# Two modulation groups of a diffusion backbone moved from between two groups of the input projection into the second of them

## The chip, the cores and the metric

The kernel runs on one core of one Trainium2 chip. The metric is the device time of one execution in microseconds (us), the median of three runs. Within a core, TensorE (PE in the profile) multiplies matrices, VectorE (DVE), ScalarE (ACT) and GpSimd (POOL) work on elements, and queues move data by DMA. SyncE (SP) only issues DMAs here. Each engine takes its instructions in the order of its own program and waits for the others by semaphores.

## The reference

Two layers work on 512 latent tokens and 256 context tokens of width 1024. Each layer begins with a modulation: the conditioning vectors `c` and `c_ctx` go through SiLU and a matrix `w_mod` of 1024 x 6144, which gives shift, scale and gate for the mixer and again for the experts. The normalised and modulated tokens `h` are then multiplied by `w_in` (1024 x 1536), and the columns of the product feed pooling, a spatial gating unit and attention:

```python
sh1, sc1, g1, sh2, sc2, g2 = modulation(c, w_mod[l], b_mod[l])
hl = modulate(x, sh1, sc1)
zl = hl @ w_in[l]
ql = apply_rope(rms_norm(heads(zl, OFF_Q, N_HEADS), q_g[l]), cos, sin)
kl = apply_rope(rms_norm(heads(zl, OFF_K, N_KV_HEADS), k_g[l]), cos, sin)
attn_l = block_attention(ql, jnp.concatenate([kl, kc], axis=1), jnp.concatenate([vl, vc], axis=1))
yl = mixer_output(zl, attn_l, pool_w[l], pool_scale[l], sgu_g[l], sgu_w[l], sgu_b[l], w_out[l])
```

After the mixer come a residual, a layer norm and a mixture of 16 experts. In the last layer the context tokens are only needed as keys and values.

## The kernel before

The input projection is done in three groups of 512 columns: first keys, values and the pooling columns, then the queries, then the two halves of the gating unit. `project(g, ...)` does the second and the third. It walks over eight slices k of the 1024 inputs. In each step ACT rounds the weight slice to the short format (`whi`, L223), DVE subtracts that from the weight (`wlo`, L224), and PE multiplies every tile of 128 tokens three times (L228 to L230): high by high, low by high, high by low. Layer 0 has six token tiles, so 18 products of 512 columns for each k; layer 1 has four tiles and 12 products. `whi` and `wlo` have two buffers each. The sums stay in PSUM (tiles `s`, two tiles of tokens each, `po` and `bk`) until all eight steps are done; then `evacuate` copies them, for the second group to `zq`.

While one group is multiplied, `prepare(k)` lets waiting generators take a step. During the second group these are the keys (L549 turns them into `kT`); during the third, the queries and the pooling. A query of one token tile is a chain: square (ACT L648), reduce (DVE L650), scale (DVE L191), power -0.5 (POOL L193, `qr`), multiply (DVE L653), multiply by the two rotary tables (POOL L657 and DVE L658), add (DVE L663), round (ACT L668), subtract the rounded part (DVE L669), eight transposes on PE (L675), and two copies to `qT`. After them the pooling multiplies a band matrix (L577). Attention begins with the scores (L750).

`mod_group` computes 512 columns of the modulation for both conditioning vectors. It loads two halves of `w_mod`, multiplies them in 16 matmuls (printed as two rows of four for each half's share, L153), and copies the result by ACT. A gate goes to `gpart` (L164) and its bias arrives by DMA. A shift or scale goes to `mpart` (L168), is transposed by PE in four pieces (L174) and summed by DVE (L175, L177). Two such groups stand in `mixer` between the second and the third group of the projection: in layer 0 one gate and one shift, in layer 1 two shifts.

Weights come in halves of 1 MB into a pool of four buffers (`ring`); in layer 1 a second pool of three (`ring1`) is added. SP issues the loads in the order of the program text; a load waits until its buffer has been read for the last time. The other engines' orders are made by a list scheduler, which moves instructions of one engine past each other where their data allow it.

Of the kernel before, what the change touches and what calls it, by code (L numbers as in the profile page):

```python
# [44 lines left out]
def step(gens, n=1):  # L45

    while n and gens:
        if next(gens[0], None):
            n -= 1
        else:  # L50
            gens.pop(0)


class Net:
# [185 lines left out]
    def mixer(self, l, left, prev):  # L240

        nc, a = self.nc, self.a
        last = l == DEPTH - 1
# [70 lines left out]
        def bank(t, pss):  # L314
            if t < LT and t % 2 == 0:
                s2 = self.P("s2")
                pss[t], pss[t + 1] = s2[:, :512], s2[:, 512:]
            elif t >= LT:
                pss[t] = self.P("po" if t == LT else "bk")

        def multiply(k, t, pss, whi, wlo):
            if k == 0:
                bank(t, pss)
            n = 256 if (last and t >= LT) else 512
            tk = slice(128 * t, 128 * t + 128)
            if last and t >= LT:
                tk = slice(128 * (t - LT), 128 * (t - LT) + 128)
                hi, lo = ctx["hi"][:, k, tk], ctx["lo"][:, k, tk]
            else:
                hi, lo = self.cat(0, k, tk), self.cat(1, k, tk)  # L330
            self.mm3(pss[t][:, :n], hi, lo, whi[:, :n], wlo[:, :n], k == 0, k == KC - 1)

        raw1 = []
# [131 lines left out]
            for t in range(NT):  # L465
                evacuate(t, pss[t], 512 if t < LT else 256)

        def project(g, raw, prepare, evacuate):

            toks = list(range(LT if last else NT))  # L470
            pss = {}
            for k in range(KC):
                prepare(k)
                whi = self.T(wl, [128, 512], "whi", F32R, bufs=2)
                wlo = self.T(wl, [128, 512], "wlo", F32R, bufs=2)
                self.split(raw[k], whi, wlo)
                for t in toks:
                    multiply(k, t, pss, whi, wlo)
            for t in toks:
                evacuate(t, pss[t], 256 if (last and t >= LT) else 512)  # L480

# [20 lines left out]
        others = []  # L502
        if l == 0:
            others = [(l, g) for g in (4, 5, 6, 7, 8, 9)]
        else:
            others = self.spare
# [174 lines left out]
        early = [keys()]  # L681
# [5 lines left out]
        def evac1(t, ps, n):  # L687
# [2 lines left out]
                at["zq"] = self.T(pool, [128, NT, 512], "zq", bufs=1)  # L690
            plain(at["zq"])(t, ps, n)

        project(1, raw1, lambda k: step(early, 1), evac1)
        zq = at["zq"]
        ge = at["ge"] = self.T(pool, [128, NT, 512], "x12")
        band = at["band"] = self.T(pool, [128, 4, 5, 128], "y12")
        nc.gpsimd.dma_start(band, a["band"])
        for m in others[2:4] if last else others[1:3]:
            self.mod_group(*m)
        qT = {}  # L700
        early += [queries(t, qT, zq) for t in range(LT if last else NT)] + [pooling(*st) for st in streams]

        def evac2(t, ps, n):
            nc.scalar.activation(ge[:, t, :], ps, AF.Gelu_apprx_tanh)

        project(2, self.load_cols("w_in", l, 2, 0), ahead, evac2)
        step(early, 1000)
        wl_stack.close()
# [1116 lines left out]
```

## Time and profile before

| | us |
|---|---|
| median of three runs | 1758.88 (1757.2 to 1763.34) |
| the profiled execution | 1761.27 |
| its span in the profile | 1759.4 |
| PE busy | 1597.1 (91%) |
| DVE busy | 620.7 (35%) |
| ACT busy | 399.8 (23%) |
| POOL busy | 334.8 (19%) |

The span is the time from the first to the last instruction that the profiler saw. The change touches about 60 us of each layer: in layer 0 from about 93 us (the second group's fourth step) to 156 us, in layer 1 from about 1034 to 1093 us. The sums over the whole span say little on these; the rows further down are taken from them.

### The profile page before, as it was taken

Reading aid. Unit: us, or ns where it says so; the run is one execution under the profiler, and the core shown is the slowest. Engines: PE = TensorE matmul, PEld = TensorE weight load, DVE = VectorE, ACT = ScalarE, POOL = GpSimd, SP = SyncE. Lnnn points to the kernel's source line nnn. Section 1 sums busy time; section 2 is a strip of 40 time slices with the busy share of each in tenths; the row PEclk is TensorE's granted clock in tenths of the full one; section 3 lists DMA queues with packets and bytes.
Section 4 is the critical chain, followed back from the end, with each engine's and each line's share of the span. In section 5 each row is a group of like instructions: output and inputs, shape, how many; then the busy total and the mean of one; then the engine's idle time right before and its main releaser. Section 6 shows DMA issues by size and latency. Waiting matters only on the chain. (4 is left out here: it accounts for less than half of the span.)

```text
span 1759.4 us, 26138 instructions
## 1 busy us (share of the span) xinstructions
PE 1597.1 (91%) x10855; PEld 835.3 (47%) x10855; DVE 620.7 (35%) x1323; ACT 399.8 (23%) x766; POOL 334.8 (19%) x354
## 2 busy tenths in 40 slices
PE   6989999987899999999998788999599988988896
PEld 3767775763444444444443566877333322222222
DVE  4543663583111111111112945657522222122214
ACT  3333664143000000000001644653400001000001
POOL 2423210022211211211211432201101100101002
PEclk9999999997999999999999798999799999999998
DMA  9441008558999999999998554054899999999994
GB/s 332 152 173 49 1 25 317 188 227 312 368 400 400 392 400 399 391 401 400 391 400 292 196 205 146 1 198 180 321 407 408 408 409 409 408 409 409 408 409 193
DMA packets 159550, 525.09 MB, mean 298 GB/s; under 512 B 10517, under 2 KB 13589, under 8 KB 159177
## 3 DMA queue, kind: packets, MB, share of 16 engines
q1 hardware_dynamic: 146116, 487.37, 71.2%
q0 software_dynamic: 10720, 27.46, 5.3%
q10 hardware_dynamic: 2596, 8.59, 1.2%
q8 instruction: 86, 1.41, 0.3%
q14 instruction: 32, 0.25, 0.0%
HBM read 504.52 MB, written 18.87 MB: 297 GB/s over the span
## 5 line engine op out<-in xcount | busy, mean ns | idle before, releaser
L1330 PE MATMUL h<-ring,xT 128*64 128x512 f32 x1448 | 331.7, 602 | 22.6 <-DMA ring<-in_w 19.7
L1330 PEld LDWEIGHTS h<-ring,xT 128*64 128x64 f32 x1448 | 98.9, 137 | 228.0 <-issue 182.1
L1330 PE MATMUL y<-ring,gpart 128*64 128x512 f32 x792 | 182.1, 603 | 9.8 <-DMA ring<-in_w 8.2
L229 PE MATMUL s<-wlo,cat 128*128 128x512 f32 x352 | 143.1, 407 | 7.8 <-DVE wlo L224 7.5
L228 PE MATMUL s<-whi,cat 128*128 128x512 f32 x352 | 144.3, 412 | 5.2 <-ACT whi L885 2.5
L1330 PE MATMUL h<-cat,xT 128*64 128x512 f32 x600 | 138.5, 603 | 5.8 <-DMA cat<-in_w 5.4
L230 PE MATMUL s<-whi,cat 128*128 128x512 f32 x352 | 141.7, 403 | 0.5 <-POOL cat L433 0.5
L1640 POOL DMA_INDIRECT acc<-y,rows x32 | 51.2, 1601 | 393.3 <-DVE y L1639 393.0
L1330 PEld LDWEIGHTS y<-ring,gpart 128*64 128x64 f32 x792 | 54.7, 138 | 126.7 <-issue 110.2
L1349 ACT ACTIVATE hT<-tr 128x64 f32<-128x64 f32 x34 | 7.3, 225 | 415.6 <-DVE hT L1351 414.3
L1349 ACT ACTIVATE gpart<-tr 128x256 f32<-128x256 f32 x32 | 12.3, 384 | 310.2 <-DVE gpart L1351 310.1
L1330 PEld LDWEIGHTS h<-cat,xT 128*64 128x64 f32 x600 | 40.8, 138 | 88.3 <-issue 71.7
L229 PEld LDWEIGHTS s<-wlo,cat 128*128 128x128 f32 x352 | 68.0, 193 | 26.6 <-DVE wlo L224 10.8
L228 PEld LDWEIGHTS s<-whi,cat 128*128 128x128 f32 x352 | 67.8, 194 | 25.9 <-issue 3.9
L753 DVE TENSOR_REDUCE am<-s 128x1 f32<-128x768 f32 (+1 forms) x68 | 65.9, 969 | 34.7 <-PE s L750 34.4
L1435 DVE SCALAR_TENSOR_TENSOR half<-y,gates,g 64x512 f32<-64x512 f32 x28 | 21.0, 750 | 161.2 <-PE y L1330 160.9
L1330 PE MATMUL c<-ring,xT 128*32 128x256 f32 x1344 | 77.6, 380 | 0.0
L750 PE MATMUL s<-kT,qT 128*128 128x256 f32 (+1 forms) x288 | 70.8, 367 | 5.9 <-ACT zq L765 5.5
L230 PEld LDWEIGHTS s<-whi,cat 128*128 128x128 f32 x352 | 68.1, 194 | 15.7 <-POOL cat L433 0.9
L765 ACT ACTIVATE zq<-s,anm 128x768 f32<-128x768 f32 (+1 forms) x80 | 65.0, 816 | 28.0 <-DVE anm L755 27.5
L153 PE MATMUL bk<-ring,cc 128*32 128x512 f32 x384 | 50.7, 645 | 20.4 <-DMA ring<-in_w_mod 19.8
L799 PE MATMUL po<-y,Z 128*64 128x128 f32 x832 | 66.9, 285 | 2.1 <-DVE zt L816 2.1
(346 smaller groups left out, 2189.9 us busy)
## 6 DMA issues: line engine op xcount, KB each, us to landing
ring<-in_w SPq DMA_DIRECT2D x280, 1024.0 KB, 19.0
cat<-in_w SPq DMA_DIRECT2D x104, 1024.0 KB, 19.2
ring<-in_w_mod SPq DMA_DIRECT2D x48, 1024.0 KB, 8.1
ring<-in_w_in SPq DMA_DIRECT2D x12, 1024.0 KB, 8.1
ring<-in_w_out SPq DMA_DIRECT2D x8, 1024.0 KB, 10.6
tab<-nn ACTq DMA_DIRECT2D x10, 512.0 KB, 7.2
acc<-res ACTq DMA_DIRECT2D x6, 512.0 KB, 4.2
fin<-acc SPq DMA_DIRECT2D x6, 512.0 KB, 4.8
```

The source lines that it names most:

```text
L153: nc.tensor.matmul(ps[32 * t:32 * t + 32, :], self.sil[:, o:o + 32], wm[k], start=k < 4, stop=k >= 4)
L228: nc.tensor.matmul(ps, ahi, bhi, start=start, stop=False)
L229: nc.tensor.matmul(ps, ahi, blo, start=False, stop=False)
L230: nc.tensor.matmul(ps, alo, bhi, start=False, stop=stop)
L750: nc.tensor.matmul(sp[:, nk * m + b0:nk * m + b1], qT[t][:, 2 * j + h, :], kT[:, 2 * h + x, k0 + b0:k0 + b1], start=x == 0, stop=x == 1)
L753: nc.vector.tensor_reduce(mx, sp[:, :nk * n].rearrange("p (m k) -> p m k", k=nk), axis=AX.X, op=OP.max)
L765: nc.scalar.activation(pbuf[:, i % 3, nk * m:nk * m + nk], sp[:, nk * m:nk * m + nk], AF.Exp, bias=nm[:, m:m + 1], scale=QK_SCALE, accum_o ...
L799: nc.tensor.matmul(po[t][64 * h:64 * h + 64, 128 * j:128 * j + 128], Z0[:, c0 + c, 128 + 64 * h:192 + 64 * h], pT[:, 128 * c:128 * c + 128 ...
L1330: self.nc.tensor.matmul(outs[s][o:o + cap, :], stat[s][:, k, :], w[k][:, n * t:n * t + n], start=k == 0, stop=k == KC - 1)
L1349: nc.scalar.activation(o[:, r], pv[:, r], AF.Copy)
L1435: nc.vector.scalar_tensor_tensor(ys[j][(r + odd) % 2][p], y[p], gates[p, e:e + 1], g2[odd][p], op0=OP.mult, op1=OP.mult)
L1640: nc.gpsimd.indirect_dma_start(out=self.acc[l, s], out_offset=bass.IndirectOffsetOnAxis(ap=rows[:, e:e + 1], axis=0), in_=y, in_offset=Non ...
```

## The change

`project` takes a list of modulation groups and works one off after step k = 3 and one after step k = 5. The second group of the projection gets the two that stood behind it.

```diff
--- before.py
+++ after.py
@@ -465,8 +465,10 @@
             for t in range(NT):
                 evacuate(t, pss[t], 512 if t < LT else 256)
 
-        def project(g, raw, prepare, evacuate):
-
+        def project(g, raw, prepare, evacuate, mods=()):
+
+
+            mods = list(mods)
             toks = list(range(LT if last else NT))
             pss = {}
             for k in range(KC):
@@ -476,6 +478,8 @@
                 self.split(raw[k], whi, wlo)
                 for t in toks:
                     multiply(k, t, pss, whi, wlo)
+                if k in (3, 5) and mods:
+                    self.mod_group(*mods.pop(0))
             for t in toks:
                 evacuate(t, pss[t], 256 if (last and t >= LT) else 512)
 
@@ -690,13 +694,11 @@
                 at["zq"] = self.T(pool, [128, NT, 512], "zq", bufs=1)
             plain(at["zq"])(t, ps, n)
 
-        project(1, raw1, lambda k: step(early, 1), evac1)
+        project(1, raw1, lambda k: step(early, 1), evac1, others[2:4] if last else others[1:3])
         zq = at["zq"]
         ge = at["ge"] = self.T(pool, [128, NT, 512], "x12")
         band = at["band"] = self.T(pool, [128, 4, 5, 128], "y12")
         nc.gpsimd.dma_start(band, a["band"])
-        for m in others[2:4] if last else others[1:3]:
-            self.mod_group(*m)
         qT = {}
         early += [queries(t, qT, zq) for t in range(LT if last else NT)] + [pooling(*st) for st in streams]
```

The scheduler orders the engines anew. At the three places below the names end in running numbers, which differ between the two files; line numbers above 468 are four higher in the changed file within `mixer`.

PE in layer 0, after the products of the second group's fourth step (`bk_681` is the PSUM tile of the sixth token tile, `s_157` that of the first two). Before:

```order
L228 MATMUL bk_681<-whi_740,cat_208 128x512
L229 MATMUL bk_681<-wlo_741,cat_208 128x512
L230 MATMUL bk_681<-whi_740,cat_209 128x512
L549 MATMUL bk_762<-ident_70,zq_735 128x128 x4
L549 MATMUL bk_768<-ident_70,zq_735 128x128 x2
L228 MATMUL s_157_663<-whi_772,cat_205 128x512
L229 MATMUL s_157_663<-wlo_773,cat_205 128x512
```

And now:

```order
L228 MATMUL bk_681<-whi_740,cat_208 128x512
L229 MATMUL bk_681<-wlo_741,cat_208 128x512
L230 MATMUL bk_681<-whi_740,cat_209 128x512
L153 MATMUL bk_766<-ring_762,cc_66 32x512 x4
L153 MATMUL bk_766<-ring_764,cc_66 32x512 x4
L553 MATMUL bk_778<-ident_70,zq_735 128x128 x4
L228 MATMUL s_157_663<-whi_788,cat_205 128x512
L229 MATMUL s_157_663<-wlo_789,cat_205 128x512
L553 MATMUL bk_784<-ident_70,zq_735 128x128 x2
```

The first modulation group (L153) stands between two steps of the group, and the transposes of the keys move a little into the next step.

DVE in layer 0 at the first two queries of the third group (`qv_947` and `qr_949` belong to the first query, `qs_1000` and `qv_1002` to the second; `wlo_1028` is the weight part of the third group's second step). Before:

```order
L650 TENSOR_REDUCE qs_945<-zt_943 128x8
L561 COPY zq_890<-po_677 128x512
L191 TENSOR_SCALAR qv_947<-qs_945 128x8
L653 TENSOR_TENSOR zq_890<-zq_890,qr_949 128x512
L658 TENSOR_TENSOR zt_943<-zq_890,rt_639 128x512
L650 TENSOR_REDUCE qs_1000<-zt_998 128x8
L663 TENSOR_TENSOR zt_952<-zt_952,zt_943 128x512
L191 TENSOR_SCALAR qv_1002<-qs_1000 128x8
```

And now:

```order
L654 TENSOR_REDUCE qs_945<-zt_943 128x8
L565 COPY zq_929<-po_677 128x512
L191 TENSOR_SCALAR qv_947<-qs_945 128x8
L657 TENSOR_TENSOR zq_929<-zq_929,qr_949 128x512
L224 TENSOR_TENSOR wlo_1028<-ring_939,whi_1027 128x512
L662 TENSOR_TENSOR zt_943<-zq_929,rt_639 128x512
L654 TENSOR_REDUCE qs_1000<-zt_998 128x8
L667 TENSOR_TENSOR zt_952<-zt_952,zt_943 128x512
L191 TENSOR_SCALAR qv_1002<-qs_1000 128x8
```

The subtraction for `wlo_1028`, which stood behind the second query's operations, has moved between the first query's two multiplications.

DVE in layer 1, from the second query's multiplication (by `qr_8175`) to the third's (by `qr_8220`); `qq_8135` is the first query's rounded part, `qq_8182` the second's. Before:

```order
L653 TENSOR_TENSOR zq_8065<-zq_8065,qr_8175 128x512
L175 TENSOR_REDUCE cols_1450_8088<-bk_8111 128x8
L561 CAST qT_8138<-bk_8139 128x512
L177 TENSOR_TENSOR cols_1450_8088<-cols_1450_8088,bcol_75 128x8
L658 TENSOR_TENSOR zt_8169<-zq_8065,rt_7864 128x512
L650 TENSOR_REDUCE qs_8216<-zt_8214 128x8
L663 TENSOR_TENSOR zt_8178<-zt_8178,zt_8169 128x512
L191 TENSOR_SCALAR qv_8218<-qs_8216 128x8
L224 TENSOR_TENSOR wlo_8244<-ring_1457_8118,whi_8243 128x512
L653 TENSOR_TENSOR zq_8065<-zq_8065,qr_8220 128x512
```

And now:

```order
L657 TENSOR_TENSOR zq_8110<-zq_8110,qr_8175 128x512
L673 TENSOR_TENSOR qq_8135<-zt_8131,qq_8135 128x8x64
L662 TENSOR_TENSOR zt_8169<-zq_8110,rt_7864 128x512
L224 TENSOR_TENSOR wlo_8289<-ring_1457_8118,whi_8288 128x512
L565 CAST qT_8138<-bk_8139 128x512
L667 TENSOR_TENSOR zt_8178<-zt_8178,zt_8169 128x512
L654 TENSOR_REDUCE qs_8216<-zt_8214 128x8
L224 TENSOR_TENSOR wlo_8357<-ring_1458_8120,whi_8356 128x512
L673 TENSOR_TENSOR qq_8182<-zt_8178,qq_8182 128x8x64
L191 TENSOR_SCALAR qv_8218<-qs_8216 128x8
L657 TENSOR_TENSOR zq_8110<-zq_8110,qr_8220 128x512
```

The sums of the modulation (L175, L177) are gone from here, and two weight subtractions and two query subtractions have come in between the same two multiplications.

## Rows read from the trace of the kernel before

**Rows 1.** Busy us (count) of PE, PEld, DVE, ACT, POOL; granted clock; DMA; GB/s
```profile
112.00:125.00 13.00, 7.77 (x50) 3.85 (x45) 8.81 (x16) 5.69 (x10) 7.27 (x5) 0.87 0.83 301
125.00:156.00 31.00, 27.97 (x148) 22.39 (x148) 18.64 (x32) 10.13 (x18) 14.01 (x8) 1.00 0.14 44
```
**Rows 2.** Timeline of PE, layer 0: start, us, instruction [idle before it <-releaser]
```profile
56.37 1.92 PE L153 MATMUL bk<-ring,cc 128*32 128x512 f32 x16
58.22 1.22 PE L305 MATMUL bk<-ident,xh 128*128 128x128 f32 x6
...
111.85 3.64 PE L153 MATMUL bk<-ring,cc 128*32 128x512 f32 x32
118.84 0.66 PE L174 MATMUL bk<-ident,mpart 128*128 128x128 f32 x4 [3.35 <-ACT mpart L168]
120.95 1.23 PE L675 MATMUL bk<-ident,qq 128*128 128x128 f32 x8 [1.45 <-DVE qq L669]
...
124.54 0.50 PE L229 MATMUL s<-wlo,cat 128*128 128x512 f32 x1 [0.43 <-DVE wlo L224]
...
150.91 0.80 PE L675 MATMUL bk<-ident,qq 128*128 128x128 f32 x8
151.54 0.46 PE L228 MATMUL s<-whi,cat 128*128 128x512 f32 x1
...
155.79 2.41 PE L577 MATMUL bk<-y,Z 128*64 128x128 f32 x40
```
**Rows 3.** Timeline of PE, layer 1
```profile
1034.55 0.63 PE L549 MATMUL bk<-ident,zq 128*128 128x128 f32 x6
...
1047.81 1.93 PE L153 MATMUL bk<-ring,cc 128*32 128x512 f32 x16
1050.45 0.66 PE L174 MATMUL bk<-ident,mpart 128*128 128x128 f32 x4 [0.72 <-ACT mpart L168]
...
1055.22 0.50 PE L229 MATMUL s<-wlo,cat 128*128 128x512 f32 x1 [1.59 <-DVE wlo L224]
...
1076.58 0.87 PE L675 MATMUL bk<-ident,qq 128*128 128x128 f32 x8
...
1092.74 0.39 PE L230 MATMUL s<-whi,cat 128*128 128x512 f32 x1
1092.97 0.94 PE L750 MATMUL s<-kT,qT 128*128 128x512 f32 x4
```
**Rows 4.** Timeline of DVE, layer 0
```profile
114.35 0.69 DVE L653 TENSOR_TENSOR zq<-zq,qr 128x512 f32<-128x512 f32 x1 [1.79 <-POOL qr L193]
115.08 0.69 DVE L658 TENSOR_TENSOR zt<-zq,rt 128x512 f32<-128x512 f32 x1
...
119.51 0.69 DVE L653 TENSOR_TENSOR zq<-zq,qr 128x512 f32<-128x512 f32 x1 [1.78 <-POOL qr L193]
...
120.72 1.79 DVE L658 TENSOR_TENSOR zt<-zq,rt 128x512 f32<-128x512 f32 x1
...
144.63 0.69 DVE L653 TENSOR_TENSOR zq<-zq,qr 128x512 f32<-128x512 f32 x1 [0.56 <-POOL qr L193]
```
**Rows 5.** Timeline of POOL, both layers
```profile
112.66 1.66 POOL L193 TENSOR_TENSOR qr<-qv,mh 128x8 f32<-128x8 f32 x1 [24.54 <-DVE qv L191]
...
120.28 1.68 POOL L657 TENSOR_TENSOR zt<-zq,rt 128x512 f32<-128x512 f32 x1 [0.81 <-DVE zq L653]
...
132.32 2.12 POOL L193 TENSOR_TENSOR qr<-qv,mh 128x8 f32<-128x8 f32 x1 [1.49 <-DVE qv L191]
...
1058.20 1.30 POOL L657 TENSOR_TENSOR zt<-zq,rt 128x512 f32<-128x512 f32 x1 [0.87 <-DVE cols L175]
```
**Rows 6.** Timeline of DVE, layer 1
```profile
1051.18 0.69 DVE L653 TENSOR_TENSOR zq<-zq,qr 128x512 f32<-128x512 f32 x1 [1.78 <-POOL qr L193]
...
1071.34 0.69 DVE L653 TENSOR_TENSOR zq<-zq,qr 128x512 f32<-128x512 f32 x1 [0.57 <-POOL qr L193]
...
1075.83 0.69 DVE L669 TENSOR_TENSOR qq<-zt,qq 128x512 fp32r<-128x512 f32 x1 [0.15 <-ACT qq L668]
```
**Rows 7.** Tile ring, 1030 to 1060 us: from issue to landing of its loads
```profile
DMA to landing us min/median/max: 5.1/9.7/14.4
```

## The prediction

> **What bounds the kernel now.** I read the granted clocks first, then the busy time by stretch, then the timelines of TensorE (PE), VectorE (DVE) and GpSimd (POOL) around the two places where the second group of the input projection meets the third. [rows 1]: in layer 0 PE is busy 7.77 of the 13 us at the boundary, and 27.97 of the 31 us after it. So there is idle time for the change to win, and it is small: PE rows of layer 0 show waits of 3.35, 1.45 and 0.43 us [rows 2], of layer 1 0.72 and 1.59 us [rows 3]. That is 7.5 us of 1759.
>
> What ends those waits matters more than their size. After the boundary six queries (four in layer 1) go through a chain that alternates between engines: DVE makes the mean square, POOL raises it to the power -0.5 (L193, "qr"), DVE multiplies (L653), POOL and DVE each multiply by a table (L657, L658), DVE adds (L663), ACT rounds (L668), DVE subtracts (L669), and PE turns the result (L675). PE holds the turns in its fixed order among the products of the third group, so it can't run ahead of this chain. The L653 of the first and the last query of layer 0 start at 114.35 and 144.63 [rows 4]: five turns of the chain in 30.3 us, 6.1 each. The 18 products between the last turn and the pooling take 155.79 - 151.54 = 4.25 us, 0.236 each [rows 2]; a step of the loop with one turn (0.63) is thus 4.9 us. The chain is slower than the products. It bounds this stretch, and it can only start when the second group has ended.
>
> **The change part by part.** E is the start of the row after the last product of the second group: 111.85 in layer 0, 1047.81 in layer 1.
>
> *The second group grows.* Both modulation groups now stand in it. One costs 58.22 - 56.37 = 1.85 us of PE where it already stands among products today [rows 2], its four transposes half of a query's eight, 0.3 to 0.4. Layer 0 has one group with transposes: 2 x 1.85 + 0.4 = 4.1. Layer 1 has two: 2 x 1.85 + 2 x 0.4 = 4.5. Nothing hides this: PE goes from product to product there, and everything behind (copies of the queries' inputs, chain, products) moves by it. ACT copies and DVE sums of the groups fall into time in which these two wait for PE; I cost them at nothing, up to 0.3 if they catch a split.
>
> *Loads.* The order of SP's queue is the same. The second half of the second group's weights no longer takes the buffer that the last splits free, but one that the first modulation group frees, so it goes out when that has been multiplied, in layer 1 at 1034.55 + 1 = 1035.6, and is wanted half of the remaining four steps later, (1047.81 - 1034.55) / 2 = 6.6 [rows 3], plus the first group's 2.25 and half of the second's 1.85: 1034.55 + 9.8 = 1044.3. That leaves 8.7 us. Loads of that window land after 5.1 to 14.4, median 9.7 [rows 7], and the 14.4 belong to a queue with more loads in it. I take 0; the bounds are 0 and 5. The third group's weights go out earlier too and are no wait any more.
>
> *The boundary.* The 7.5 us of waits go, and the products of the third group start at once. Then the chain is late. I follow DVE's new order from E' (the new E), with starts of full-width DVE operations 0.6 to 0.65 apart, ACT's rounding 0.65, POOL's power 1.66 where DVE is idle beside it and 2.0 to 2.1 where DVE works on two tiles ([rows 5]: 1.66 and 2.12), POOL's multiplication 1.30 alone and 1.68 beside DVE [rows 5], and 0.25 from the small scaling to the power. One thing is to be seen in [rows 4, 5]: L658 takes 0.69 where it starts just before POOL's multiplication, and 1.79 where it starts 0.4 us into one (120.72 against POOL's 120.28 to 121.96); it ends 0.55 after POOL does. Call that held.
>
> Layer 0, from one L653 to the next (L657 in the changed file's numbering):
> first: L653 0.7, a split of a weight (new here) 0.6, L658 held behind it 1.8, reduce 0.6, add 0.6, scaling 0.1, gap 0.25, power 1.66 = 6.35 (before 119.51 - 114.35 = 5.16);
> second: L653, subtract, L658 held, add, copy, reduce, subtract, scaling, gap, power 2.0 = 7.9;
> third: L653, L658, a split that is held, add, reduce, scaling, gap, power 2.1 = 6.85;
> fourth: L653, copy, L658 held (1.45), reduce, add, scaling, gap, power 2.0 = 6.3;
> fifth: L653, subtract, reduce, a split held (1.0), copy, scaling, gap, power 2.1 = 6.05.
> Sum 33.4, against 30.3. The first L653 stays at E + 2.5, so the last stands at E' + 35.9; POOL 1.3, ACT 0.65, DVE 0.65 and gaps make 3.6 to the last turn at 39.5, and turn and 16 products 0.63 + 3.8 lead to the pooling at E' + 43.9. Before: 155.79 - 111.85 = 43.94. **Layer 0: +4.1 + 43.9 - 43.9 = +4.1 us.** What the boundary gave, PE waits out at the turns.
>
> Layer 1: the first L653 at E' + 4.1 (before 1051.18 - 1047.81 = 3.37; a split stands ahead of the scaling), then 5.65, 8.8 (L658 held, two splits, copy, add, reduce and subtract between two powers) and 6.3: the last at 24.85 (before 1071.34 - 1047.81 = 23.5) [rows 6]. A subtract of another query, POOL, L658 held, a split, a copy, add, ACT and the subtract make 6.25 to 31.1; turn at 31.2. From the last turn to the first scores before are 1092.97 - 1076.58 = 16.4 us [rows 3], with 39 products; 18 are left now: 16.4 - 21 x 0.23 = 11.6. End at E' + 42.8, before 45.16. **Layer 1: +4.5 - 2.4 = +2.1 us.** Here the products that PE has ahead win a part back.
>
> Sum +6.2 on the profiled execution's 1761.27 (span 1759.4 and 1.9 around it): 1767.5. That execution lies 2.4 above the median of the runs, 1758.88; on the median I predict **1765**. What stands outside the two stretches has the same order and moves along.
>
> Where I chose: the turns of the chain. From below, no product waits at all: layer 0 4.1 + 108 x 0.236 + 6 x 0.63 - 43.9 = -10.5, layer 1 4.5 + 96 x 0.23 + 4 x 0.63 + 6.6 (pooling) - 45.2 = -9.5. DVE would have to finish a query in under 5 us, which no row shows before the last turn. From above, each turn as long as the longest (8.8): 5 x 8.8 - 33.4 = 10.6 more in layer 0. I take the sums above, which are made of rows.
>
> That DVE is held has a rule behind it. The Trainium skill, "SBUF — State Buffer", section "SBUF: two separate sides", says VectorE and GpSimd share a port pair as an exclusive lock: with two SBUF inputs on VectorE, whichever starts first keeps it for its whole instruction, the other blocks. The trace agrees (1.79 against 0.69). It speaks against the change, since four more operations than before start late enough to be blocked; were the 1.79 an accident of that row, each would take 0.69 and the sum would be about +2 instead of +6.
>
> **The rivals.** *A, the boundary simply closes*: the 7.5 us of waits go and nothing takes their place, since the groups cost PE the same wherever they stand: 1758.9 - 7.5 = 1751. For it: [rows 1] shows 5.2 idle us in one stretch. Against it: the chain's first step needs the end of the second group, and that is later. It decides if the chain's turns fall to PE's 4.9 us; this is the case on the other side.
> *B, a draw*: the chain keeps the old pace, 30.3 in layer 0 and the old offsets in layer 1: +4.1 - 3.1 = +1.0, and 4.5 + 28.8 + 0.1 + 11.6 - 45.2 = -0.2 (28.8 is 1075.83 + 0.69 less 1047.81 [rows 6]): +0.8, 1760. For it: DVE does the same work. Against it: the order in which it does it.
> *C, weights late in layer 1*: my +6.2 and up to 5 more, 1770. Against it: that load is first in its queue now.
> That the groups don't land where the change says is no rival: the order shows them there.
>
> **How the numbers follow.** A change under 0.3% (5.3 us) can't be told from none by a measurement of this kernel. Forecast 0.55, its own range 1762 to 1769 (1.5 us of error in each layer's chain); 0.40 of it is slower, 0.15 same. A 0.13 (0.12 faster, 0.01 same). B 0.24 (0.22 same, 0.02 slower). C 0.08, slower. Faster 0.12, same 0.38, slower 0.50. The range runs from below B, 1756, to C, 1770, and leaves out most of A and the worst of C, under 0.2.
>
> **What would show it.** In the changed profile: the second group's last product 4 to 4.5 us later; no wait for a modulation copy or for the third group's weights; PE idle before the query turns instead (about 4 us before the first, in layer 0); the first pooling product of layer 0 near 160 and the first scores of layer 1 about 6 later than 1093. Held DVE operations of 1.5 to 1.9 us among L662 and the splits. I am wrong if the pooling of layer 0 starts at or before 155.8, or if PE's waits for the turns of layer 0 don't grow.

## The result, and the profile after

The changed kernel takes 1769.77 us (median of 9 runs, 1768.65 to 1771.93), the kernel before 1759.06 in its runs beside it: ratio 1.0060, 95% interval 1.0046 to 1.0074, so 8.1 to 13.0 us slower. The prediction was 1765, range 1756 to 1770. The direction and the mechanism were right; the loss, 10.7 us by the medians, is larger than the 6.2 of the sum.

The profiled execution has a span of 1769.9 (before 1759.4). PE's timeline, both layers; it answers to [rows 2, 3]:

```profile
94.69 1.93 PE L153 MATMUL bk<-ring,cc 128*32 128x512 f32 x16
...
106.04 1.92 PE L153 MATMUL bk<-ring,cc 128*32 128x512 f32 x16
...
117.97 0.39 PE L228 MATMUL s<-whi,cat 128*128 128x512 f32 x1
...
128.03 1.23 PE L679 MATMUL bk<-ident,qq 128*128 128x128 f32 x8 [3.76 <-DVE qq L673]
...
139.66 0.88 PE L679 MATMUL bk<-ident,qq 128*128 128x128 f32 x8 [0.85 <-DVE qq L673]
...
145.74 0.50 PE L229 MATMUL s<-wlo,cat 128*128 128x512 f32 x1 [1.00 <-DVE wlo L224]
148.57 0.88 PE L679 MATMUL bk<-ident,qq 128*128 128x128 f32 x8 [2.32 <-DVE qq L673]
...
156.61 0.87 PE L679 MATMUL bk<-ident,qq 128*128 128x128 f32 x8 [0.79 <-DVE qq L673]
...
161.13 2.40 PE L581 MATMUL bk<-y,Z 128*64 128x128 f32 x40
...
306.56 1.07 PE L153 MATMUL bk<-ring,cc 128*32 128x512 f32 x8 [1.11 <-DMA ring<-in_w_mod]
...
318.53 0.80 PE L228 MATMUL s<-whi,cat 128*128 128x512 f32 x1 [3.28 <-ACT whi L887]
...
1059.87 0.50 PE L228 MATMUL s<-whi,cat 128*128 128x512 f32 x1
...
1090.35 0.79 PE L679 MATMUL bk<-ident,qq 128*128 128x128 f32 x8
...
1103.67 1.95 PE L752 MATMUL s<-kT,qT 128*128 128x512 f32 x8 [1.63 <-ACT x L706]
```

In layer 0 the groups (L153) stand at 94.69 and 106.04 inside the second group, whose end has moved from 111.85 to 117.97. No wait for a modulation copy is left, as forecast. Instead PE waits 3.76 us before the first turn of a query (L679; 1.45 before) and 0.85, 1.00, 2.32 and 0.79 at later places, and the pooling (L581) starts at 161.13 against 155.79. In layer 1 the second group ends at 1059.87 (before 1047.81), and the first scores (L752) start at 1103.67 (before 1092.97).

Busy time of PE, PEld, DVE, ACT and POOL with counts, granted clock, DMA share and GB/s, in the two stretches that answer to [rows 1]:

```profile
118.00:131.00 13.00, 9.10 (x39) 7.03 (x38) 9.37 (x15) 4.21 (x9) 6.53 (x4) 0.82 0.00 2
131.00:161.00 30.00, 25.04 (x120) 19.61 (x118) 19.63 (x31) 9.72 (x18) 14.02 (x8) 0.91 0.11 36
```

The idle time of the boundary has shrunk from 5.2 to 3.9 us, that of the stretch behind it has grown from 3.0 to 5.0. The granted clock there fell from 1.00 (2.4 GHz throughout) to 0.91 (parts of it at 1.2 GHz), behind the idle time ahead of the turns.

The chain, DVE's timeline in layer 0 and POOL's, which answer to [rows 4, 5]:

```profile
120.56 0.69 DVE L657 TENSOR_TENSOR zq<-zq,qr 128x512 f32<-128x512 f32 x1 [1.78 <-POOL qr L193]
121.17 0.68 DVE L224 TENSOR_TENSOR wlo<-ring,whi 128x512 fp32r<-128x512 f32 x1
121.77 1.79 DVE L662 TENSOR_TENSOR zt<-zq,rt 128x512 f32<-128x512 f32 x1
...
126.59 0.69 DVE L657 TENSOR_TENSOR zq<-zq,qr 128x512 f32<-128x512 f32 x1 [1.75 <-POOL qr L193]
...
127.80 1.79 DVE L662 TENSOR_TENSOR zt<-zq,rt 128x512 f32<-128x512 f32 x1
...
153.02 0.69 DVE L657 TENSOR_TENSOR zq<-zq,qr 128x512 f32<-128x512 f32 x1 [1.53 <-POOL qr L193]
```

```profile
121.40 1.61 POOL L661 TENSOR_TENSOR zt<-zq,rt 128x512 f32<-128x512 f32 x1 [0.88 <-DVE zq L657]
...
127.42 1.62 POOL L661 TENSOR_TENSOR zt<-zq,rt 128x512 f32<-128x512 f32 x1 [0.87 <-DVE zq L657]
```

The split (L224) now stands between L657 and L662. So L662 starts at 121.77, when POOL's product of 121.40 to 123.01 is running, takes 1.79 instead of 0.69, and ends 0.55 after POOL. Among the queries layer 0 has five such operations of full width where it had one, layer 1 three where it had two.

### The profile page after: what moved, and what is told of

Read it like the earlier page. It is cut to its first block, busy times and chain, and to the rows that moved or that the text cites. A ratio compares the mean times of both kernels' runs of the same rounds, so it can differ in the third digit from the quotient of the medians.

```text
span 1769.9 us, 26138 instructions
## 1 busy us (share of the span) xinstructions
PE 1599.3 (90%) x10855; PEld 838.0 (47%) x10855; DVE 622.6 (35%) x1323; ACT 399.3 (23%) x766; POOL 334.0 (19%) x354
## 5 line engine op out<-in xcount | busy, mean ns | idle before, releaser
L752 PE MATMUL s<-kT,qT 128*128 128x256 f32 (+1 forms) x288 | 70.7, 367 | 7.5 <-ACT zq L767 5.8
L153 PE MATMUL bk<-ring,cc 128*32 128x512 f32 x384 | 51.1, 647 | 21.2 <-DMA ring<-in_w_mod 20.7
```

The costliest lines, as they stand in the source:

```text
L153: nc.tensor.matmul(ps[32 * t:32 * t + 32, :], self.sil[:, o:o + 32], wm[k], start=k < 4, stop=k >= 4)
L752: nc.tensor.matmul(sp[:, nk * m + b0:nk * m + b1], qT[t][:, 2 * j + h, :], kT[:, 2 * h + x, k0 + b0:k0 + b1], start=x == 0, stop=x == 1)
```

## The experiments

Times are medians of the runs of five rounds, with the ratio to the kernel before and its 95% interval. The kernel before, beside them, had 1759.04 (e1 to e4), 1758.50 (e5 to e8) and 1760.42 (e9 to e12). "Stage" is what a profile shows from the start of the second group to the first scores, against the profile of before.

One thing moves layer 0's stage without any edit. In all fourteen profiles PE waits 2.2 to 2.4 us for a split near 84 us, in the second group. In nine (before, after, e1, e5, e7 to e11) the seven or eight products behind this wait run at 1.2 GHz (0.63 us each instead of 0.39; granted clock 0.86 from 80 to 92 us), in the other five at 2.4 GHz (1.00). The group takes 39.1 us in the profile of before and 37.7 in e2's, which has the same order there: 1.4 us.

**One layer alone.** e1 gives the second group its modulation groups in layer 0 only, e2 in layer 1 only.

```diff
-        project(1, raw1, lambda k: step(early, 1), evac1, others[2:4] if last else others[1:3])
+        project(1, raw1, lambda k: step(early, 1), evac1, () if last else others[1:3])   # e1
+        for m in others[2:4] if last else ():                                           # e1, at the old place
+            self.mod_group(*m)
```

> Only layer 0 has its two groups inside the second group's products; layer 1 is as before. Chain theory: the query chain of layer 0 starts at the second group's end, about 4.75 us later, and runs 43.2 us from there to the pooling (43.94 before): about +4.0 us in time, layer 1's stage +0. If the +1.6 us that the changed kernel lost between 299 and 430 us (loads around the output projection) belong to the new rotation of weight buffers in layer 0, then +5.6 and the same late load is seen here; if they are chance, the profile lacks it. Closed-boundary rival: 5.2 us of waits in layer 0 vanish, about -5.

> Only layer 1 has its two groups inside the second group's products. Chain theory: second group's end 5.1 us later, first scores 43.8 us behind it instead of 45.2: about +3.8 us, and layer 0's stage +0, with no late load near 300 us. With the layer 0 run the two sum to about 7.8; the whole change measured 10.7, so if the sum of the two runs is near 10.7 the rest belongs to one of the layers, if it is near 8 the rest is chance or needs both. Closed-boundary rival: about -2.3.

Measured: e1 1765.93 (+6.9; ratio 1.0037, 1.0023 to 1.0050), e2 1763.98 (+4.9; 1.0030, 1.0018 to 1.0041). Both layers lose; the sum, 11.8, is near the whole change. The edited stages are +4.0 in e1's profile and +4.25 in e2's; the unedited ones are -0.1 (layer 1 of e1) and -1.4 (layer 0 of e2, the clock above). The five turns of layer 0 take 32.4 us in e1 as in the changed kernel (L657 from 120.12 to 152.54). The late load near 300 us, which the changed kernel shows at 306.56, is missing in e1, and e2 has it with layer 0 as before:

```profile
298.61 1.06 PE L153 MATMUL bk<-ring,cc 128*32 128x512 f32 x8 [1.17 <-DMA ring<-in_w_mod]
```

So it does not belong to layer 0's groups.

**Groups in the third group.** e3 hands the same list to `project(2, ...)`, so the second group ends as early as before.

```diff
-        project(1, raw1, lambda k: step(early, 1), evac1, others[2:4] if last else others[1:3])
+        project(1, raw1, lambda k: step(early, 1), evac1)
-        project(2, self.load_cols("w_in", l, 2, 0), ahead, evac2)
+        project(2, self.load_cols("w_in", l, 2, 0), ahead, evac2, others[2:4] if last else others[1:3])
```

> Both groups stand inside the third group's products (after steps 3 and 5) instead of the second's. The second group then ends as early as before (111.85 and 1047.81), and PE does the groups while the chain makes it wait. Chain theory: pooling of layer 0 at E + 43.2 (the chain as in the changed kernel), -0.8; layer 1's scores at E + 43.8 less up to 1.6, -1.4 to -3: together -2 to -4 us. If the products and not the chain set the pace, all waits at the boundary go: -7.5. If the groups cost their 9.8 us of PE wherever they stand and the chain's waits do not hide them: about 0 or slower.

Measured: 1764.37 (+5.3; 1.0031, 1.0016 to 1.0045). A miss. PE and DVE of e3, layer 0:

```profile
143.78 2.39 PE L153 MATMUL bk<-ring,cc 128*32 128x512 f32 x16
...
149.69 0.79 PE L679 MATMUL bk<-ident,qq 128*128 128x128 f32 x8
...
154.60 1.92 PE L153 MATMUL bk<-ring,cc 128*32 128x512 f32 x16
...
158.03 2.40 PE L581 MATMUL bk<-y,Z 128*64 128x128 f32 x40
```

```profile
112.99 0.70 DVE L657 TENSOR_TENSOR zq<-zq,qr 128x512 f32<-128x512 f32 x1 [1.79 <-POOL qr L193]
113.60 0.69 DVE L224 TENSOR_TENSOR wlo<-ring,whi 128x512 fp32r<-128x512 f32 x1
114.20 1.80 DVE L662 TENSOR_TENSOR zt<-zq,rt 128x512 f32<-128x512 f32 x1
...
145.42 0.69 DVE L657 TENSOR_TENSOR zq<-zq,qr 128x512 f32<-128x512 f32 x1 [1.53 <-POOL qr L193]
```

I had the groups stand in PE's waits for the turns. The scheduler put the first at 143.78, ahead of the fifth turn (146.10), and the second at 154.60, behind the last (149.69), where PE has nothing to wait for and it costs its full time; in layer 1 both stand there (1078.18 and 1090.26, the turn at 1077.45). The stages are +1.3, or +2.7 without the clock's part, and +2.7. But the chain part held: its first L657 comes 3.75 us after the second copy of the queries, as in the kernel before, and still its five turns take 145.42 - 112.99 = 32.4 us, not 30.3. With the second group's end unmoved, that separates the two causes: a later start, and a longer chain by the new order on DVE (again the split ahead of L662, held for 1.80).

**One group of two.** e4 moves only the group after k = 3.

```diff
-                if k in (3, 5) and mods:
+                if k == 3 and mods:
-        project(1, raw1, lambda k: step(early, 1), evac1, others[2:4] if last else others[1:3])
+        project(1, raw1, lambda k: step(early, 1), evac1, others[2:3] if last else others[1:2])
+        for m in others[3:4] if last else others[2:3]:   # at the old place
+            self.mod_group(*m)
```

> Only the first of the two groups (the gate in layer 0, a shift in layer 1) stands inside the second group's products, after step 3; the other stays between second and third group. Chain theory: the second group ends 1.9 to 2.2 us later in layer 0 and 2.5 in layer 1, and everything behind follows the chain: +2 to +2.5 and +1 to +2.5, about +4 us in all, half of the whole change. If the loss came from the two groups together (loads, buffers), this one is near 0; closed-boundary rival: about -3.

Measured: 1761.86 (+2.8; 1.0016, 1.0005 to 1.0026). About a quarter of the whole, not half; still 4 is inside the interval (0.9 to 4.6), and the rival's -3 is not. The stages are +0.6, or +2.0 without the clock's part, as expected of layer 0, and +0.3.

**Without the chain.** e5 (kernel before) and e6 (changed kernel) turn the queries as they are.

```diff
         def queries(t, qT, zq):
             z = zq[:, t]
-            ...
+            o3 = z.rearrange("p (h d) -> p h d", d=64)
             qq = self.T(pool, [128, 8, 2, 64], "qq", F32R, bufs=1)
```

> The kernel before with the query chain cut: queries are neither normalised nor rotated (left out; only the rounding, its subtraction and the turn stay). Chain theory: the waits for the turns of the third group go (3.0 us in layer 0, 2.5 in layer 1), those at the boundary for the modulation copy stay (3.35 and 0.72): about -5.5 us, 1753.5. If the turns were not what PE waited for, about 0.

> The changed kernel with the same cut (queries neither normalised nor rotated). Chain theory: without the chain the third group runs at PE's pace in both kernels, so moving the groups saves the boundary's waits: 4 to 6 us faster than the cut kernel before, about 1748 to 1750. If the loss lies in the groups themselves or their loads (a group costs more among the products than at the boundary), it is still slower than the cut kernel before, by 6 to 10 us.

Measured: e5 1744.78 (0.9916, 0.9895 to 0.9937), e6 1743.37 (0.9913, 0.9894 to 0.9933). The 10.7 us between the two kernels are gone: -1.4 by the medians, and the two ratios allow some 5 us either way. PE's turns in layer 0, e5 and then e6, and e6's stretch of 30 us by busy time:

```profile
116.67 0.65 PE L174 MATMUL bk<-ident,mpart 128*128 128x128 f32 x4 [0.72 <-ACT mpart L168]
117.08 0.88 PE L656 MATMUL bk<-ident,qq 128*128 128x128 f32 x8
119.48 0.73 PE L228 MATMUL s<-whi,cat 128*128 128x512 f32 x2 [1.52 <-ACT whi L223]
```

```profile
115.50 0.85 PE L660 MATMUL bk<-ident,qq 128*128 128x128 f32 x8
...
120.13 0.80 PE L660 MATMUL bk<-ident,qq 128*128 128x128 f32 x8
...
139.41 0.80 PE L660 MATMUL bk<-ident,qq 128*128 128x128 f32 x8
```

```profile
115.00:145.00 30.00, 30.00 (x170) 24.87 (x170) 12.15 (x19) 11.34 (x20) 0.00 (x0) 1.00 0.11 36
```

PE is busy 30.00 of 30 us, a turn every 4.8. The gain of 4 to 6 is not seen, though the intervals don't exclude it: without the chain the kernel before has little left to save at the boundary, 0.72 and 1.52 instead of 3.35, 1.45 and 0.43. The stages agree: together e6's are 3.6 us shorter than e5's, of which 1.4 is the clock, and 2.2 are left. Those waits were the chain's too: [rows 2] names ACT's copy for the 3.35, but with the chain cut the same copy ends its wait after 0.72. e5's own gain was larger than the 5.5 I had worked out for the same reason.

**A shorter chain.** e7 (before) and e8 (changed) multiply by the power of -0.5 after the rotation, so that the power runs beside the products.

```diff
-            nc.vector.tensor_mul(z3, z3, r[:, :, None].to_broadcast([128, 8, 64]))
             ...
                 nc.vector.tensor_add(o, o, sq)
+            nc.vector.tensor_mul(o3, o3, r[:, :, None].to_broadcast([128, 8, 64]))
```

> The kernel before, with a query's normalisation moved behind its rotation: the table products start at once, the power of -0.5 runs beside them, and the factor is multiplied in last. Same operations and count. Chain theory: the power leaves the serial path, turns fall from 6.1 towards 5.2 us (some 8 DVE operations of 0.6 a query, one held): layer 0 -3 to -4.5, layer 1 -2 to -3, about 1752 to 1754. If POOL's order (a power between two products) still sets the turn, -1 or less.

> The changed kernel with the normalisation behind the rotation. Chain theory: turns of layer 0 fall from 6.5 to about 5.2, 5 x 1.3 = 6 us, and layer 1 by 3 to 4: about 1760, that is 9 to 10 below the changed kernel. Against the kernel before with the same edit it stays behind by up to 5 if DVE still sets the turns, and gets ahead by up to 3 if PE does. If the loss is not in the turns, it stays 8 to 10 behind.

Measured: e7 1753.87 (0.9973, 0.9961 to 0.9986), e8 1755.48 (0.9979, 0.9966 to 0.9992). e7 as expected; e8 gains 14 on the changed kernel where I expected 9 to 10, and the distance falls to 1.6.

**No held operations.** e9 (changed) and e10 (before) move the first table product of the queries from POOL to DVE.

```diff
-                nc.gpsimd.tensor_mul(o3, z3, rt[:, 0, 0, t:t + 1, :].to_broadcast([128, 8, 64]))
+                nc.vector.tensor_mul(o3, z3, rt[:, 0, 0, t:t + 1, :].to_broadcast([128, 8, 64]))
-                nc.gpsimd.tensor_mul(o3, z3, qkg[:, 0:1, :].to_broadcast([128, 8, 64]))
+                nc.vector.tensor_mul(o3, z3, qkg[:, 0:1, :].to_broadcast([128, 8, 64]))
```

> The changed kernel with the queries' first table product moved from POOL to DVE: DVE gets 0.61 us more per query, no DVE operation is held behind a POOL product any more, and the sum need not wait for POOL. Theory (held operations lengthen the turns): turns of layer 0 5.65, 6.65, 7.75, 5.4 and 5.05 = 30.5 against 32.5 measured, layer 1 about 1.5 less: 3 to 4 us below the changed kernel, about 1766. If being held costs nothing on the path, DVE's extra work makes it slower than the changed kernel, by up to 10 x 0.6 = 6: 1772 to 1776.

> The kernel before with the same product on DVE. It had one held multiplication (1.79) in layer 0 and one in layer 1 besides a split: little to win, 0.6 to pay per query, sums no longer waiting 0.5 for POOL: 1757 to 1760. The prediction's own figure for a world without held operations was that the change costs about 2 us: then the changed kernel with this edit is 2 above this one, not 10.7. If the turns' length has another cause, the distance stays at 8 or more.

Measured: e9 1757.09 (0.9990, 0.9979 to 1.0001), e10 1758.31 (0.9990, 0.9978 to 1.0001). With DVE doing more, the changed kernel loses 12.7 us of its time and stands level with the kernel before. DVE and PE of e9, layer 0:

```profile
119.64 0.69 DVE L657 TENSOR_TENSOR zq<-zq,qr 128x512 f32<-128x512 f32 x1 [1.78 <-POOL qr L193]
120.24 0.68 DVE L224 TENSOR_TENSOR wlo<-ring,whi 128x512 fp32r<-128x512 f32 x1
120.85 0.69 DVE L661 TENSOR_TENSOR zt<-zq,rt 128x512 f32<-128x512 f32 x1
121.45 0.69 DVE L662 TENSOR_TENSOR zt<-zq,rt 128x512 f32<-128x512 f32 x1
...
149.94 0.69 DVE L657 TENSOR_TENSOR zq<-zq,qr 128x512 f32<-128x512 f32 x1 [1.81 <-POOL qr L193]
```

```profile
154.11 0.86 PE L679 MATMUL bk<-ident,qq 128*128 128x128 f32 x8
...
155.66 2.40 PE L581 MATMUL bk<-y,Z 128*64 128x128 f32 x40
```

Every full-width operation takes 0.68 or 0.69. The turns are 5.52, 6.67, 7.70, 5.42 and 4.99 = 30.3, where 30.5 was worked out. That is 2.2 us of the changed kernel's 32.5; in layer 1 the turns go from 20.0 to 18.6. The rest of the 12.7 is not the held time itself: the scheduler also placed PE's products anew, 3 instead of 16 between the last turn and the pooling (154.11 to 155.66, against 156.61 to 161.13), 3 us in layer 0, and the wait of 1.63 ahead of layer 1's scores is gone. e9 does not part these from one another. Its two stages are together 9.1 us shorter than the changed kernel's; what lies outside them is not explained.

**Both edits.** e11 (before) and e12 (changed) have the late normalisation and both products on DVE.

```diff
-                nc.gpsimd.tensor_mul(o3, z3, ...)
+                nc.vector.tensor_mul(o3, z3, ...)   # in the version of e7 and e8
```

> The kernel before with the normalisation behind the rotation and both table products on DVE, so that POOL does nothing but the power. Chain theory: the waits of 3.8 us at the first turn of layer 0 (DVE's sum behind POOL's product) and of 0.4 to 0.6 at later ones go: some 3 us below the kernel with late normalisation alone (1753.9), about 1750 to 1751, the version that beats both. If DVE's 0.6 more per query makes it the bound (8 operations of 0.6 and copies: 5.4 a turn), it is no faster than 1754.

> The changed kernel with the same two edits. Chain theory: with the shortest chain PE sets most turns, so the moved groups save what the boundary still waits and cost nothing: within 2 us of the same edits on the kernel before, either way, about 1749 to 1753. If the groups' place itself costs the time, 8 to 10 above it.

Measured: e11 1751.67 (0.9958, 0.9943 to 0.9973), e12 1754.90 (0.9972, 0.9961 to 0.9983). e11 beats both kernels, the one before by 8.8 us by the medians and 0.42%, or 7.4 us, by the ratio. PE of e11, layer 0:

```profile
119.25 1.10 PE L675 MATMUL bk<-ident,qq 128*128 128x128 f32 x8 [0.97 <-DVE qq L669]
...
125.74 0.80 PE L675 MATMUL bk<-ident,qq 128*128 128x128 f32 x8
...
150.00 2.40 PE L577 MATMUL bk<-y,Z 128*64 128x128 f32 x40
```

The first turn waits 0.97, later ones not at all, and the pooling starts at 150.00. Moving the groups then costs 3.2 us by the medians, a little over the 2 expected, and far from 8 to 10. Against what I had expected, PE does not set most turns in e12: it waits 2.51 us for a split in layer 0 (133.60) and 4.12 for a turn in layer 1 (1060.79).

## Why the prediction was right in kind and short in size

| term | predicted | measured |
|---|---|---|
| layer 0: second group grows | 4.1 | 4.9 |
| last copies to first L657, counted from E' | 2.5 | 2.6 |
| five turns | 6.35, 7.9, 6.85, 6.3, 6.05 = 33.4 | 6.03, 7.88, 6.66, 6.09, 5.80 = 32.5 |
| last L657 to pooling | 8.0 | 8.1 |
| layer 0, net | +4.1 | +4.1 |
| layer 1: second group grows | 4.5 | 5.1 |
| E' to first L657, three turns | 4.1, 20.75 | 3.75, 20.0 |
| last L657 to scores | 18.0 | 20.0 |
| layer 1, net | +2.1 | +3.7 |
| outside the two stages | 0 | +2.7 |

The measured terms leave out what the two profiles were already apart at the start of each stage (1.25 and 6.98). The loss is thus the growth of the second group, 4.9 and 5.1, of which the stages behind it gave back 0.8 and 1.4.

Two things were luck. Layer 0's net is right to the tenth because two errors cancel: the group was taken 0.8 us too short and the turns 0.9 too long. And the range held only by its upper end, 1770, which stood for the late weights of rival C; the forecast's own range, 1762 to 1769, ended below the 1769.77.

*The boundary's waits* went and came back at the turns, as forecast: 7.5 us of waits gave nothing. The prediction's list left out waits for turns that the kernel before already had. In layer 0:

```profile
133.01 0.89 PE L675 MATMUL bk<-ident,qq 128*128 128x128 f32 x8 [0.18 <-DVE qq L669]
...
139.24 0.88 PE L675 MATMUL bk<-ident,qq 128*128 128x128 f32 x8 [1.15 <-DVE qq L669]
...
145.98 0.88 PE L675 MATMUL bk<-ident,qq 128*128 128x128 f32 x8 [1.71 <-DVE qq L669]
```

In layer 1 they were 1.61 and 0.87. With them PE waited 8.3 us from the second group's end to the pooling of layer 0 and 4.8 to the scores of layer 1; now it waits 8.9 and 9.2. Rival A is ruled out by the result, B too (8.1 to 13.0, against +0.8; its 28.8 is 28.7 when worked out, which changes little), and C did not come: none of PE's waits from layer 1's second group to its scores names a load.

*The chain* was the step that decided, and it is shown, not only argued. Cutting it removes the loss (e5, e6), shortening it nearly does (e7, e8), and its length follows from durations of single operations to within 0.4 us a turn. From the second group's end to the pooling layer 0 takes 43.9 us before, 43.2 in the changed kernel and 29.1 with the chain cut (e6), where the prediction's sum from below has 108 x 0.236 + 6 x 0.63 = 29.3. The length of the turns alone is not the loss: in layer 1 the three turns take 20.0 us, before 1071.34 - 1051.18 = 20.2, and the loss is nearly as large.

*Held operations*: where L662 or a split starts inside a POOL product it ends 0.54 to 0.56 us after it, in all eight cases of the changed kernel. The rule of the Trainium skill ("SBUF — State Buffer", section "SBUF: two separate sides") that one engine keeps the shared port for a whole instruction agrees with these rows. In e9, with no POOL product to run into, no operation is held and the turns fall to the sum without holds. But in e10, where nothing is held either, the five turns of layer 0 take 32.4 us, as long as the changed kernel's, and its stages are 0.6 and 2.0 shorter than before. So the holds are shown as a part of the changed kernel's turns, not as the cause of the loss. The prediction's figure for such a world, +2, takes off layer 0's holds alone (some 4.4 us by its own terms); by my estimate the two that it names in layer 1, some 1.1 each, bring it to about 0. Measured is -1.2 by the medians of e9 and e10; their ratios are equal to four places with intervals of 0.0011 either way, so +2 is not excluded, and 10.7 is.

*What was mis-sized.* First, a group among products costs more than the 1.85 of its matmuls and 0.4 of its transposes: about 2.4 to 2.55 (half of 4.9 and of 5.1). Each change between products and other matmuls leaves about 0.1 us (94.37 to 94.69 is 0.32, where products follow at 0.23), and 0.2 of layer 0's 4.9 is one product more at 1.2 GHz. Second, layer 1's end: 11.6 us from the last turn to the scores, measured 13.3. ACT's timeline of the changed kernel there:

```profile
1100.59 0.63 ACT L599 ACTIVATE cat<-Z 128x512 fp32r<-128x512 f32 x1 [2.16 <-DVE Z L589]
1101.24 1.28 ACT L706 ACT_TABLE_LOAD   x1
1102.54 2.07 ACT L706 ACTIVATE x<-s 128x512 f32<-128x512 f32 x4
```

The scores wait 1.63 for the activation L706, which frees their PSUM, and that one waits for a table load of 1.28 behind the rounding of the second pooling (L599). Before, the load lay at 1088.43, and PE had 31 products between the second pooling and the scores to run meanwhile; now only 10 were left, and the load lies on the path. I counted those 10 products and not what ACT had to do beside them.

Third, 2.7 us lie outside: +1.25 before 30 us, where the order is that of before, +1.8 between 280 and 428 us (PE waits 1.11 for a modulation load at 306.56, and for the split weight 3.28 at 318.53 against 2.48 before), and -0.4 elsewhere. Over the twelve other profiles the first stretch differs from the profile of before by -0.5 to +1.3 and the second by -2.2 to +1.7, in no order with the edits, and the late load shows in five of them (e2, e4, e5, e8, e9), so one profile can't lay this on the change. That e1's median exceeds its stage by 2.9 speaks for a small part of it being real; its interval (4.0 to 8.8) begins where the stage alone lies. This stays open.

## What to carry to other kernels

A wait at a boundary is worth what the next bound leaves of it: before filling it, write down which chain starts at that boundary and whether the filler delays its start. A bubble in which the slower chain already runs costs nothing; work put ahead of the chain delays the chain by its full time, here 4.9 and 5.1 us, of which 0.8 and 1.4 came back. And a schedule is compared by its slowest chain's order, operation by operation: one weight split moved between two multiplications lengthened the first turn here from 5.2 to 6.0 us, and to 5.5 where POOL had no product to hold the second one (e9).

## What had not been expected of the hardware

A power on POOL does not hold DVE as a product does. DVE and POOL of e7:

```profile
129.90 0.68 DVE L666 TENSOR_TENSOR zt<-zt,qr 128x512 f32<-128x512 f32 x1
130.50 0.68 DVE L224 TENSOR_TENSOR wlo<-ring,whi 128x512 fp32r<-128x512 f32 x1
```

```profile
129.19 1.63 POOL L193 TENSOR_TENSOR qr<-qv,mh 128x8 f32<-128x8 f32 x1
```

An operation with two inputs starts at 130.50 and one at 129.90, both inside the power of 129.19 to 130.82, and both take 0.68. A product also holds smaller work: the scaling L191, which takes 0.16 or 0.17 where no product runs beside it, took 0.85 at 142.04 in the kernel before, inside POOL's product of 141.55 to 142.85. The other way round DVE holds the power: begun during an operation with two inputs it takes 2.01 instead of 1.64 (132.34 in the changed kernel, behind the split of 132.17). The Trainium skill's rule of the shared port, in the section named above, gives it to the engine that starts first for its whole instruction; for products that is what the rows show, for this power they do not.
